# Layer 0's second half in one fixed order: retention, out-projection, norm and routing woven together, GpSimd's arithmetic moved to VectorE

## The chip, the core and the metric

The kernel runs on one core of a Trainium2 chip. The time is that of one execution on the device, in microseconds. Five engines work side by side, each on its own queue: TensorE (PE, with its weight loads as PEld), VectorE (DVE), ScalarE (ACT), GpSimd (POOL) and SyncE (SP), which only issues transfers. They wait for one another through semaphores.

## The reference

Two layers of a block with 256 context and 1024 latent tokens of width 1024; each has a mixer, a residual sum, a norm and a mixture of 32 experts. The part that matters here is layer 0 behind its in-projection: retention in both directions over chunks of 128 tokens and 4 heads, its group norm with a gate, the out-projection, the residual, the second norm and the router's choice of two experts for every token.

```python
scores = einsum('bhnid,bhnjd->bhnij', q, k) * dmat
inner  = einsum('bhnij,bhnje->bhnie', scores, v)
out    = inner + einsum('bhnid,bhnde->bhnie', q_dec, s_prev)   # s_prev: state before the chunk
s      = g_chunk * s + einsum('cd,ce->de', k * w_tail, v)      # from chunk to chunk
y  = (o - mean(o)) * rsqrt(var(o) + EPS) * gn_w * silu(gate)   # by head
x  = x + g1 * (concat([y, fourier_mix(f)]) @ w_out)
h2 = rms_norm(x, norm2_w) * (1 + sc2) + sh2
# router: softmax and argmax over 4 groups, top 2 of 8 experts in the group, for h2
```

## The kernel before

The ten token tiles (two of context, eight latent) are at the same time the ten chunks of the retention. Layer 0's first half (layer0_a, inproj0) computes q, k, v, gate and the Fourier part, and runs the backward retention, whose states it stores (SB_d). The second half, `layer0_b` (line 828), is a loop over steps s, in which three things are called one after the other for three neighbouring tiles: `ret_chunk` for chunk s, `outproj` and `out_norm` for tile s - 1, `router` for tile s - 2, and `route_part` after tiles 2, 5, 7 and 9.

`ret_chunk` (line 894) loads k, v, q, gate, Fourier part and backward state; GpSimd scales q for both directions (qd, line 907); PE forms the scores (sc), DVE multiplies them by the decay (sm); PE adds the products with the states and with v (o); PE transposes k, DVE scales it (kd), PE forms kv, and DVE updates the forward state SF, which the next chunk needs. DVE takes mean and variance of o by head (bn_stats, bn_aggr), forms the inverse square root by integer arithmetic and three Newton steps (`rsqrt_steps`, line 280), and normalizes (y, line 931); PE transposes y, DVE multiplies by the gate, and `mix_split` writes each factor as a rounded part (mh) and a residue (ml).

`outproj` multiplies mh and ml by the split weights: two halves of 512 columns, 24 products each, the four Fourier pieces first. DVE scales by the modulation g1 (yg, line 973) and GpSimd adds x (line 974). `out_norm` squares on ACT, has a second inverse square root on DVE, then h = x * r * A2 on DVE (line 988) and + S2 on GpSimd (line 989), and stores h2, from which the experts gather their rows. `router` transposes x, multiplies by the router's weights (lgp), and scales the logits by the same r; `route_part` turns the logits of two or three tiles into lists for the experts: many small DVE operations and a few small matmuls (rk, ls).

The order of the instructions on each engine is left to the framework's scheduler: it takes what its model says is ready, earlier calls first. Layer 1's first part does it otherwise: there `Ordered` (line 105) keeps PE, DVE and ACT in the order of the calls and keeps a model of the engines' times (`cost`, line 118), and `Weave` (line 208) runs several generators in steps between the products: at each `pump` it takes the first part by priority whose next step is ready by that model, and `until` lets PE's modelled time pass when none is. The experts (`moe`) follow layer 0's second half; their first gather needs the lists of the last `route_part`.

Of the kernel before, what the change touches and what calls it, by code (L numbers as in the profile page):

```python
# [19 lines left out]
P = 128  # L20
D = 1024
# [80 lines left out]
class Ordered:  # L102
# [13 lines left out]
    def cost(self, eng, op, out, ins, func):  # L116
        n = int(np.prod(out.shape[1:]))
        if eng != "tensor":
            n = max([n] + [int(np.prod(x.shape[1:])) for x in ins])
        if eng == "tensor":  # L120
            return max(n, 128 if ins[0].dtype == F32 else 64) * (2 if ins[0].dtype == F32 else 1) / 2400
        if eng == "vector":
            wide = any(x.dtype in (F32, F32R, I32) for x in [out, *ins])
            return 0.067 + n / 960 * (1.0 if wide else 0.5)
        if eng == "scalar":
            c = 0.02 + n / 1060
            if func is not None and func not in self.PLAIN and func != self.table:
                self.table = func
                c += 1.3
            return c  # L130
        return 0.2 + n / 480
# [128 lines left out]
class Emit:  # L260
# [565 lines left out]
            self.nc.vector.scalar_tensor_tensor(out=new[:, h, :], in0=old[:, h, :], scalar=self.gch[:, 4 * d + h:4 * d + h + 1], in1=kv[:, h, :], op0=OP.mult, op1=OP.add)  # L826

    def layer0_b(self):
        tc, nc, t = self.tc, self.nc, self.t
        pool = lambda s, **k: s.enter_context(tc.tile_pool(reuse_waits="tile", **k))  # L830
        with ExitStack() as st:
            b1 = pool(st, name="b1", bufs=1)
            wk = pool(st, name="wk", bufs=2)
            ps = pool(st, name="bps", bufs=1, space=PSUM)
            self.SF = None
            m, o = {}, {}
            for s in range(12):
                if s < 10:
                    m[s] = self.ret_chunk(wk, ps, s)
                if s == 0:  # L840
                    drain(self.load_wout(b1, t["even_w_out"][0], self.wsc, (2,)))
                    self.mid_setup(0, b1)
                if 0 < s < 11:
                    drain(self.out_rows(0, wk, 1 if s < 3 else 0))
                    x = self.outproj(0, wk, ps, s - 1, *m.pop(s - 1))
                    drain(self.out_norm(0, wk, s - 1, x))
                    o[s - 1] = x
                if s > 1:
                    drain(self.router(0, wk, ps, s - 2, o.pop(s - 2), s - 2, 1 if s < 4 else 0))
                    if s - 2 in (2, 5, 7, 9):  # L850
                        drain(self.route_part(ps, *{2: (0, 3, "kv"), 5: (3, 3, "kv"), 7: (6, 2, "kv"), 9: (8, 2, "sc")}[s - 2]))
        self.b0.close()
        self.hst.close()

# [36 lines left out]
        self.modset = self.rset = None  # L891
        self.rn = {}

    def ret_chunk(self, wk, ps, n):

        nc = self.nc
        v = nc.vector
        kT, vv = self.load_kv(self.wk0, n)
        qT = self.chunk_T(self.wk0, self.qT_d, n, "qT")
        gT = self.chunk_T(self.wk0, self.gT_d, n, "gT")  # L900
        fT = self.chunk_T(self.wk0, self.yT_d, n, "fT")
        SB = self.flat(self.wk0, self.SB_d[n], "SBt") if n != 1 else None
        SF = self.SF
        qd = self.wk0.tile([P, 2, 4, P], F32, name="qd", tag="qd", bufs=1)
        for d, S in ((0, SF), (1, SB)):
            if S is not None:
# [5 lines left out]
        v.tensor_tensor(out=sm, in0=sc, in1=self.DS, op=OP.mult)  # L912
        o = ps.tile([P, 4, P], F32, name="o", tag="o")
        for h in range(4):
            l = [(qd[:, d, h, :], S[:, h, :]) for d, S in ((0, SF), (1, SB)) if S is not None] + [(sm[:, h, :], vv[:, h, :])]
            for i, (a, b) in enumerate(l):
                nc.tensor.matmul(o[:, h, :], lhsT=a, rhs=b, start=(i == 0), stop=(i == len(l) - 1))
        if n < 9:
            kv = self.ret_kv(self.wk0, ps, kT, vv, 0)
# [3 lines left out]
        s6 = wk.tile([P, 4, 6], F32, name="s6", tag="s6")  # L923
        mv = wk.tile([P, 4, 2], F32, name="mv", tag="mv")
        for h in range(4):
            v.bn_stats(out=s6[:, h, :], in_=o[:, h, :])
            v.bn_aggr(out=mv[:, h, :], in_=s6[:, h, :])
        r = self.rsqrt(wk, mv[:, :, 1], 4, "gn")
        y = wk.tile([P, 4, P], F32, name="y", tag="sm", bufs=2)
        for h in range(4):  # L930
# [5 lines left out]
        return self.mix_split(wk, gT, fT)  # L936

    def mix_split(self, wk, a, b):
        nc = self.nc
# [53 lines left out]
    def router(self, layer, wk, ps, i, x, n, which):  # L993

        nc = self.nc
        v = nc.vector
        if self.rset != which:
            self.rset = which
            self.wra, self.rk = self.wr, self.rb
            if layer == 0:  # L1000
                self.wra, self.rk = self.modp.tile([P, KD, 36], F32, name="wra"), self.modp.tile([P, 36], F32, name="rk")
            lg = ps.tile([P, 36], F32, name="lgk", tag=self.tags["lg"][0], bufs=self.tags["lg"][1])
            for k in range(KD):
                nc.tensor.matmul(lg, lhsT=self.S2c[:, layer, which, k:k + 1].to_broadcast([P, P]), rhs=self.wr[:, k, :], start=(k == 0), stop=(k == KD - 1))
# [12 lines left out]
        for k in range(KD):  # L1017
            nc.tensor.matmul(lg, lhsT=xT[:, k, :], rhs=self.wra[:, k, :], start=(k == 0), stop=(k == KD - 1))  # L1018
        v.scalar_tensor_tensor(out=self.lgt[:, i, :], in0=lg, scalar=self.rn.pop(n), in1=self.rk, op0=OP.mult, op1=OP.add)
# [1308 lines left out]
```

## Time and profile before

| | us |
|---|---|
| three runs | 2817.58, 2820.12, 2822.80 (median 2820.12) |
| profiled execution | 2826.72 |
| its span | 2825.0 |
| PE busy | 2549.0 (90%) |
| DVE busy | 2282.9 (81%) |
| ACT busy | 1526.6 (54%) |
| POOL busy | 628.7 (22%) |
| mean granted clock of PE | 0.947 |

Times in the rows are counted from the span's start. A granted clock of 1.00 stands for 2.4 GHz and 0.50 for 1.2 GHz; a mean between them is a mixture. Matmuls overlap in the pipeline, so the pace of PE is read from one start to the next and not from the duration of one. A matmul of f32 operands appears as two instructions. In brackets stands how long the engine had been idle before an instruction, and who released it.

### The profile page before, as it was taken

Reading aid. Unit: us, or ns where it says so; the run is one execution under the profiler, and the core shown is the slowest. Engines: PE = TensorE matmul, PEld = TensorE weight load, DVE = VectorE, ACT = ScalarE, POOL = GpSimd, SP = SyncE. Lnnn points to the kernel's source line nnn. Section 1 sums busy time; section 2 is a strip of 40 time slices with the busy share of each in tenths; the row PEclk is TensorE's granted clock in tenths of the full one; section 3 lists DMA queues with packets and bytes.
Section 4 is the critical chain, followed back from the end, with each engine's and each line's share of the span. In section 5 each row is a group of like instructions: output and inputs, shape, how many; then the busy total and the mean of one; then the engine's idle time right before and its main releaser. Section 6 shows DMA issues by size and latency. Waiting matters only on the chain.

```text
span 2825.0 us, 40970 instructions
## 1 busy us (share of the span) xinstructions
PE 2549.0 (90%) x14733; PEld 2103.9 (74%) x14733; DVE 2282.9 (81%) x4243; ACT 1526.6 (54%) x2097; POOL 628.7 (22%) x543
## 2 busy tenths in 40 slices
PE   6999998986999999994899999989869999999980
PEld 3777787775778888883878788888757888888870
DVE  5688867676899999896858888487769999999877
ACT  3332121111778888884856644111227888888871
POOL 0001334333111222111213222113321111111114
PEclk8999999897999999997999999999969999999995
DMA  8455866334999999997636334785369999999884
GB/s 292 140 185 209 321 218 198 130 127 166 335 365 359 382 377 377 377 377 260 209 122 194 125 134 143 271 277 177 105 249 340 361 365 381 376 380 377 289 321 179
DMA packets 417356, 746.46 MB, mean 264 GB/s; under 512 B 50792, under 2 KB 137960, under 8 KB 414960
## 3 DMA queue, kind: packets, MB, share of 16 engines
q1 hardware_dynamic: 374688, 627.38, 63.9%
q0 software_dynamic: 41296, 112.10, 10.6%
q10 hardware_dynamic: 1152, 4.19, 0.4%
q8 instruction: 121, 1.98, 0.3%
q14 instruction: 99, 0.81, 0.1%
HBM read 667.69 MB, written 109.42 MB: 275 GB/s over the span
## 4 chain that ended last, share of the span: by engine, by line
issue 25%; PE 15%; DVE 5%; POOL 5%; DMA 4%; ACT 1%; POOLq 0%; SPq 0%; ACTq 0%; another core or an unknown queue 0%; DVEq 0%
PE acc L92 5%; POOL xe L1310 2%; POOL y_d L1314 1%; DMA y_d<-ye,sidx 1%; DMA kx<-kx_d 1%; PE tp L92 1%; PE tu L92 1%; PE op L324 1%; PE op L326 1%; PE op L322 1%; POOL y L92 1%; DMA y_d<-ye,v 1%; PE lgp L1018 1%; DVE cy L92 1%; PE rs L92 0%
## 5 line engine op out<-in xcount | busy, mean ns | idle before, releaser
L92 DVE TENSOR_TENSOR mwl<-mx,mwh 128x1024 fp32r<-128x1024 f32 x320 | 383.8, 1219 | 34.8 <-ACT mwh L92 32.5
L92 DVE TENSOR_TENSOR mwl<-raw,mwh 128x1024 fp32r<-128x1024 f32 x294 | 353.6, 1219 | 37.5 <-ACT mwh L92 36.3
L92 ACT ACTIVATE mwh<-mx 128x1024 fp32r<-128x1024 f32 x320 | 324.4, 1052 | 9.1 <-DMA h_d<-h 2.3
L92 ACT ACTIVATE mwh<-raw 128x1024 fp32r<-128x1024 f32 x294 | 298.2, 1051 | 8.3 <-DMA raw<-in_moe_w_gate 4.2
L92 PE MATMUL acc<-hUh,wr 128*128 128x512 f32 (+1 forms) x768 | 239.9, 389 | 0.8 <-ACT wr L92 0.6
L1310 POOL DMA_INDIRECT xe<-h_d,gidx x64 | 109.5, 1712 | 546.0 <-PE xt L92 516.5
L92 PE MATMUL u<-mwh,xTh 128*128 128x512 f32 x512 | 212.5, 415 | 0.0
L92 PE MATMUL g<-mwh,xTh 128*128 128x512 f32 x512 | 207.5, 405 | 0.0
L92 PE MATMUL g<-mwl,xTh 128*128 128x512 f32 x512 | 202.7, 396 | 3.7 <-DVE mwl L92 3.3
L92 PE MATMUL g<-mwh,xTl 128*128 128x512 f32 x512 | 201.5, 394 | 0.0
L92 PE MATMUL u<-mwh,xTl 128*128 128x512 f32 x512 | 201.4, 393 | 0.0
L1314 POOL DMA_INDIRECT y_d<-ye,sidx x64 | 98.2, 1534 | 460.3 <-ACT ye L92 429.6
L92 PE MATMUL u<-mwl,xTh 128*128 128x512 f32 x512 | 200.1, 391 | 0.0
L92 DVE TENSOR_TENSOR mwl<-mw,mwh 128x1024 fp32r<-128x1024 f32 x146 | 177.1, 1220 | 26.3 <-ACT mwh L92 25.6
L92 PE MATMUL dn<-mwl,aTh 128*128 128x512 f32 x496 | 193.8, 391 | 0.1
L92 PE MATMUL dn<-mwh,aTh 128*128 128x512 f32 x496 | 193.6, 390 | 0.0
L92 PE MATMUL dn<-mwh,aTl 128*128 128x512 f32 x496 | 193.1, 389 | 0.0
L433 DVE SCALAR_TENSOR_TENSOR adam<-raw,cs,adam 128x1024 f32<-128x1024 f32 x112 | 140.4, 1295 | 27.5 <-ACT adam L431 26.5
L92 PEld LDWEIGHTS acc<-hUh,wr 128*128 128x128 f32 x768 | 138.2, 191 | 22.3 <-ACT wr L92 0.8
L92 ACT ACTIVATE mwh<-mw 128x1024 fp32r<-128x1024 f32 x146 | 148.7, 1052 | 4.0 <-DMA mw<-in_moe_w_gate 2.2
L92 PE MATMUL acc<-hUl,wr 128*128 128x512 f32 (+1 forms) x384 | 148.7, 387 | 0.0
L322 PE MATMUL acc<-hTh,wh 128*128 128x512 f32 (+1 forms) x384 | 138.9, 362 | 0.0
(602 smaller groups left out, 6636.9 us busy)
## 6 DMA issues: line engine op xcount, KB each, us to landing
mx<-in_moe_w_up SPq DMA_DIRECT2D x62, 1024.0 KB
raw<-in_moe_w_up SPq DMA_DIRECT2D x56, 1024.0 KB
raw<-in_moe_w_down SPq DMA_DIRECT2D x55, 1024.0 KB
mx<-in_moe_w_gate SPq DMA_DIRECT2D x54, 1024.0 KB
raw<-in_moe_w_gate SPq DMA_DIRECT2D x50, 1024.0 KB
raw<-in_ada_w SPq DMA_DIRECT2D x48, 1024.0 KB
mx<-in_moe_w_down SPq DMA_DIRECT2D x41, 1024.0 KB
mw<-in_moe_w_down SPq DMA_DIRECT2D x37, 1024.0 KB
```

What stands on the lines that cost most here:

```text
L92: r = getattr(self.engine, op)(*a, **k)
L322: a = m(ps, lhsT=lh, rhs=rh, start=start, stop=False)
L324: b = m(ps, lhsT=lh, rhs=rl, start=False, stop=False)
L326: c = m(ps, lhsT=ll, rhs=rh, start=False, stop=stop)
L433: nc.vector.scalar_tensor_tensor(out=box[i], in0=w[:, r], scalar=c, in1=box[i], op0=OP.mult, op1=OP.add)
L1018: nc.tensor.matmul(lg, lhsT=xT[:, k, :], rhs=self.wra[:, k, :], start=(k == 0), stop=(k == KD - 1))
L1310: self.gath = nc.gpsimd.indirect_dma_start(out=x, out_offset=None, in_=h2, in_offset=bass.IndirectOffsetOnAxis(ap=idx, axis=0), bounds_che ...
L1314: nc.gpsimd.indirect_dma_start(out=self.y2_d, out_offset=bass.IndirectOffsetOnAxis(ap=idx, axis=0), in_=y, in_offset=None, bounds_check=2 ...
```

## The change

`layer0_b` now runs under `Ordered` and `Weave`: the retention (priority 1), the loading of a weight piece (2), the norm (3) and the routing (4) become generators, and the loop over the tiles calls only `outproj`, with the weave's `pump` between its products. Chunk n + 1 may begin when tile n's products begin. What GpSimd computed (qd, the sum with x, the sum with S2) is computed by DVE; kd and y move from DVE to ACT, four instructions of 128 columns each. For tiles 0 to 7 the second norm's inverse square root rides as a fifth column in that of the retention two chunks later. The square's unused output becomes a bf16 scratch tile. The modelled cost of a matmul in `Ordered.cost` is raised: f32 products to twice what they were, f32r products by 13 ns, others by 3; layer 1 uses the same function.

```diff
@@ cost
-            return max(n, 128 if ins[0].dtype == F32 else 64) * (2 if ins[0].dtype == F32 else 1) / 2400
+            if ins[0].dtype == F32:
+                return max(n, 128) * (2 if op == "transpose" else 4) / 2400
+            return max(n, 64) / 2400 + (0.013 if ins[0].dtype == F32R else 0.003)
@@ layer0_b
+        nc = self.nc = Ordered(self, tc.nc)
+        wv = Weave(nc)
-            for s in range(12):
-                if s < 10:
-                    m[s] = self.ret_chunk(wk, ps, s)
-                if s == 0:
-                    drain(self.load_wout(b1, t["even_w_out"][0], self.wsc, (2,)))
-                    self.mid_setup(0, b1)
-                if 0 < s < 11:
-                    drain(self.out_rows(0, wk, 1 if s < 3 else 0))
-                    x = self.outproj(0, wk, ps, s - 1, *m.pop(s - 1))
-                    drain(self.out_norm(0, wk, s - 1, x))
-                    o[s - 1] = x
-                if s > 1:
-                    drain(self.router(0, wk, ps, s - 2, o.pop(s - 2), s - 2, 1 if s < 4 else 0))
...
+            def rets():
+                ld = {0: self.ret_load(0)}
+                for n in range(10):
+                    if n + 1 < 10:
+                        ld[n + 1] = self.ret_load(n + 1)
+                    yield from self.ret_steps(wk, ps, n, *ld.pop(n), m, mv)
+                    yield lambda n=n: n <= state["at"]
+                    yield
+
+            def norms():
+                for n in range(10):
+                    yield lambda n=n: n in o
+                    yield
+                    if n > 7:
+                        yield from self.rsqrt_tile(wk, n, mv)
+                    yield lambda n=n: n in self.rn
+                    if n in (0, 2):
...
+                    yield from self.h2_steps(wk, n, o[n])
+
+            def routes():
+                for n in range(10):
+                    yield lambda n=n: n in o
+                    yield
+                    yield from self.router(0, wk, ps, n, o[n], n, 1 if n < 2 else 0)
+                    if n in (2, 5, 7, 9):
+                        yield from self.route_part(ps, *{2: (0, 3, "lg"), 5: (3, 3, "lg"), 7: (6, 2, "lg"), 9: (8, 2, "lg")}[n])
+            self.mid_setup(0, b1)
+            ret = wv.start(rets(), 1)
+            wo = wv.start(self.load_wout(b1, t["even_w_out"][0], self.wsc, (2,)), 2)
+            norm, route = wv.start(norms(), 3), wv.start(routes(), 4)
+            for n in range(10):
...
+                wv.until(lambda: n in m)
+                if n == 0:
+                    wv.finish(wo)
+                state["at"] = n
+                x = self.outproj(0, wk, ps, n, *m.pop(n), wv.pump)
...
+                nc.scalar.activation(junk, x, AF.Square, scale=1.0 / 32, accum_out=ss)
+                o[n] = x
+            wv.finish(ret, norm, route)
@@ ret_chunk -> ret_steps (generator; a yield names what the next step waits for)
-                nc.gpsimd.tensor_tensor(out=qd[:, d], in0=qT, in1=self.rowd[:, d], op=OP.mult)
+            v.tensor_tensor(out=qd, in0=qT[:, None].to_broadcast([P, 2, 4, P]), in1=self.rowd, op=OP.mult)
...
+            for h in range(4):
+                nc.scalar.activation(kd[:, h], tp[:, h], AF.Copy, scale=self.wfb[:, h:h + 1])
...
+        yield o,
...
+        steps = self.rsqrt_steps(wk, mv[:, :, 1], 5, "gn")
+        r = yield from steps
+        if n >= 2:
+            self.rn[n - 2] = r[:, 4:5]
+        nmr = wk.tile([P, 4], F32, name="nmr", tag="nmr")
+        v.scalar_tensor_tensor(out=nmr, in0=mv[:, 0:4, 0], scalar=-1.0, in1=r[:, 0:4], op0=OP.mult, op1=OP.mult)
...
-            v.tensor_scalar(out=y[:, h, :], in0=o[:, h, :], scalar1=mv[:, h, 0:1], scalar2=r[:, h:h + 1], op0=OP.subtract, op1=OP.mult)
+            nc.scalar.activation(y[:, h, :], o[:, h, :], AF.Identity, scale=r[:, h:h + 1], bias=nmr[:, h:h + 1])
+        if n < 9:
             self.SF = wk.tile([P, 4, P], F32, name="SF", tag="SF")
             self.ret_step(self.SF, SF, kv, 0)
+        yield y, ("tp", 1)
@@ h2_steps
+        v.scalar_tensor_tensor(out=h2, in0=x, scalar=self.rn[n], in1=self.A2, op0=OP.mult, op1=OP.mult)
+        yield
+        v.tensor_tensor(out=h2, in0=h2, in1=self.S2, op=OP.add)
@@ outproj
-            nc.gpsimd.tensor_tensor(out=x[:, c], in0=y, in1=x[:, c], op=OP.add)
+            (v if layer == 0 else nc.gpsimd).tensor_tensor(out=x[:, c], in0=y, in1=x[:, c], op=OP.add)
```

## Rows read from the trace of the kernel before

**Rows 1.** Stretches of the span: busy time of each engine, clock, DMA
```profile
core 0: us, PE busy (x) PEld busy (x) DVE busy (x) ACT busy (x) POOL busy (x), PEclk, DMA share, GB/s
429.50:446.10 16.60, 14.12 (x86) 12.69 (x85) 14.49 (x39) 3.60 (x6) 3.84 (x4) 0.90 0.75 227
446.10:677.70 231.60, 206.81 (x1150) 176.97 (x1149) 168.05 (x609) 31.48 (x58) 82.41 (x62) 0.90 0.44 146
677.70:700.10 22.40, 11.41 (x69) 10.35 (x67) 15.82 (x72) 7.55 (x12) 7.49 (x8) 0.65 0.53 187
...
780.00:1270.00 490.00, 487.18 (x2307) 399.10 (x2306) 451.18 (x485) 408.03 (x485) 85.46 (x52) 1.00 1.03 373
1460.00:1820.00 360.00, 347.99 (x3487) 292.49 (x3487) 265.87 (x648) 185.92 (x345) 99.83 (x125) 1.00 0.51 169
```

**Rows 2.** Timeline of PE at the stage's head: start, us, what
```profile
429.49 1.05 PE L910 MATMUL sc<-qT,kT 128*128 128x128 f32 x8
430.38 0.39 PE L917 MATMUL o<-SBt,qd 128*128 128x128 f32 x2
...
436.55 0.72 PE L322 MATMUL op<-hTh,mh 128*128 128x512 f32 x1
```

**Rows 3.** Timeline of DVE at the stage's head
```profile
431.89 3.09 DVE L875 SCALAR_TENSOR_TENSOR wol<-raw,gw,woh 128x512 fp32r<-128x512 f32 x3
...
440.47 0.49 DVE L926 BATCH_NORM_STATS2 s<-o 128x6 f32<-128x128 f32 x2 [1.34 <-PE o L917]
...
442.44 1.23 DVE L958 SCALAR_TENSOR_TENSOR A<-A,h 128x1024 f32<-128x1024 f32 x1
...
445.35 1.37 DVE L931 TENSOR_SCALAR y<-o,mv,gn_y 128x128 f32<-128x128 f32 x4
```

**Rows 4.** Timeline of PE inside two tiles
```profile
545.25 0.63 PE L326 MATMUL op<-hTh,ml 128*128 128x512 f32 x1
...
546.53 0.63 PE L326 MATMUL op<-hTh,ml 128*128 128x512 f32 x1
...
569.97 0.39 PE L322 MATMUL op<-hTh,mh 128*128 128x512 f32 x1
...
574.73 0.39 PE L322 MATMUL op<-hTh,mh 128*128 128x512 f32 x1
577.17 0.30 PE L934 MATMUL tp<-ident,y 128*128 128x128 f32 x1 [2.05 <-DVE y L931]
```

**Rows 5.** Waits of PE from 428 to 700: us in total, times, longest
```profile
PE rk L1112 <- DVE raw L1109: 18.0, 4, 8.5
PE tp L934 <- DVE y L931: 14.2, 6, 3.3
```

**Rows 6.** Groups of DVE and POOL, 428 to 700: busy us, mean ns, idle before
```profile
L931 DVE TENSOR_SCALAR y<-o,mv,gn_y 128x128 f32<-128x128 f32 x40 | 13.8, 403 | 0.4
L295 DVE SCALAR_TENSOR_TENSOR n_x<-n_y,n_h 128x1 f32<-128x1 f32 x30 | 9.2, 305 | 0.6
L286 DVE TENSOR_SCALAR gn_x<-mv 128x4 f32<-128x4 f32 x10 | 7.3, 734 | 0.3
L815 DVE TENSOR_TENSOR kd<-tp,wfb 128x512 f32<-128x512 f32 x9 | 6.1, 680 | 0.0
L974 POOL TENSOR_TENSOR x<-yg,x 128x512 f32<-128x512 f32 x20 | 27.7, 1387 | 102.4 <-DVE yg L973 96.9 <-issue 3.7 <-DVE raw L1109 1.7
L907 POOL TENSOR_TENSOR qd<-qT,rowd 128x512 f32<-128x512 f32 x17 | 25.6, 1524 | 35.3 <-PE o L917 35.3
L989 POOL TENSOR_TENSOR h<-h,S 128x1024 f32<-128x1024 f32 x10 | 23.8, 2383 | 20.1 <-DVE h L988 15.3 <-DVE raw L1097 4.8
```

**Rows 7.** Timeline of the tail: last product, a DVE operation, first gather
```profile
677.32 0.63 PE L326 MATMUL op<-woh,ml 128*128 128x512 f32 x1
...
685.73 2.05 DVE L1082 TENSOR_TENSOR raw<-lgt,raw 128x8 f32<-128x8 f32 x1
...
700.09 1.22 POOL L1310 DMA_INDIRECT xe<-h_d,gidx  x1 [8.73 <-DVE gidx L1263]
```

**Rows 8.** Timeline of ACT in layer 1: four pieces of 128 columns
```profile
1330.66 1.49 ACT L92 ACTIVATE xn<-tp,Sc,Ac 128x128 f32<-128x128 f32 x4
```

More of the change, by code (lines that the diff above doesn't have):

```diff
@@ new lines, in layer0_b @@
+            for n in range(2):
+                mv[n] = wk.tile([P, 5, 2], F32, name="mv", tag="mv", bufs=3)
+                nc.vector.memset(mv[n][:, 4], 1.0)
+            def rets():
[6 more added lines that the diff above has]
+                    yield
@@ L852, in layer0_b @@
+            wv.finish(ret, norm, route)
+        self.nc = tc.nc
         self.b0.close()
@@ L892, in mid_setup, with ret_load, ret_steps @@
         self.rn = {}
-    def ret_chunk(self, wk, ps, n):
+    def ret_load(self, n):
+        w = self.wk0
+        kT, vv = self.load_kv(w, n)
+        qT = self.chunk_T(w, self.qT_d, n, "qT")
+        SB = self.flat(w, self.SB_d[n], "SBt") if n != 1 else None
+        fT = self.chunk_T(w, self.yT_d, n, "fT")
+        gT = self.chunk_T(w, self.gT_d, n, "gT")
+        return kT, vv, qT, SB, fT, gT
+    def ret_steps(self, wk, ps, n, kT, vv, qT, SB, fT, gT, mix, mvs):
         nc = self.nc
         v = nc.vector
[L898 to L902, printed above, removed]
         SF = self.SF
+        mv = mvs[n]
+        yield kT, qT
         qd = self.wk0.tile([P, 2, 4, P], F32, name="qd", tag="qd", bufs=1)
-        for d, S in ((0, SF), (1, SB)):
-            if S is not None:
-                nc.gpsimd.tensor_tensor(out=qd[:, d], in0=qT, in1=self.rowd[:, d], op=OP.mult)
+        if SF is not None and SB is not None:
+            v.tensor_tensor(out=qd, in0=qT[:, None].to_broadcast([P, 2, 4, P]), in1=self.rowd, op=OP.mult)
+        else:
+            d = 0 if SB is None else 1
+            v.tensor_tensor(out=qd[:, d], in0=qT, in1=self.rowd[:, d], op=OP.mult)
         sc = ps.tile([P, 4, P], F32, name="sc", tag="sc")
@@ L912, in ret_chunk @@
         v.tensor_tensor(out=sm, in0=sc, in1=self.DS, op=OP.mult)
+        if n < 9:
+            yield kT, ("tp", 1)
+            tp = ps.tile([P, 4, P], F32, name="tp", tag="tp", bufs=2)
+            for h in range(4):
+                nc.tensor.transpose(tp[:, h, :], kT[:, h, :], self.ident)
+            kd = self.wk0.tile([P, 4, P], F32, name="kd", tag="kd")
+            for h in range(4):
+                nc.scalar.activation(kd[:, h], tp[:, h], AF.Copy, scale=self.wfb[:, h:h + 1])
+        yield sm, qd, vv, ("o", 1)
         o = ps.tile([P, 4, P], F32, name="o", tag="o")
@@ L917, in ret_chunk @@
                 nc.tensor.matmul(o[:, h, :], lhsT=a, rhs=b, start=(i == 0), stop=(i == len(l) - 1))
+            if h == 1:
+                yield
         if n < 9:
-            kv = self.ret_kv(self.wk0, ps, kT, vv, 0)
+            yield kd, ("kv", 1)
+            kv = ps.tile([P, 4, P], F32, name="kv", tag="kv", bufs=1)
+            for h in range(4):
+                nc.tensor.matmul(kv[:, h, :], lhsT=kd[:, h, :], rhs=vv[:, h, :], start=True, stop=True)
+        yield o,
+        s6 = wk.tile([P, 4, 6], F32, name="s6", tag="s6")
+        for h in range(4):
+            v.bn_stats(out=s6[:, h, :], in_=o[:, h, :])
+        for h in range(4):
+            v.bn_aggr(out=mv[:, h, :], in_=s6[:, h, :])
+        yield
+        steps = self.rsqrt_steps(wk, mv[:, :, 1], 5, "gn")
[4 more added lines that the diff above has]
+        v.scalar_tensor_tensor(out=nmr, in0=mv[:, 0:4, 0], scalar=-1.0, in1=r[:, 0:4], op0=OP.mult, op1=OP.mult)
+        y = wk.tile([P, 4, P], F32, name="y", tag="sm", bufs=2)
+        for h in range(4):
+            nc.scalar.activation(y[:, h, :], o[:, h, :], AF.Identity, scale=r[:, h:h + 1], bias=nmr[:, h:h + 1])
+        if n < 9:
             self.SF = wk.tile([P, 4, P], F32, name="SF", tag="SF")
             self.ret_step(self.SF, SF, kv, 0)
[L923 to L930, printed above, removed]
-            v.tensor_scalar(out=y[:, h, :], in0=o[:, h, :], scalar1=mv[:, h, 0:1], scalar2=r[:, h:h + 1], op0=OP.subtract, op1=OP.mult)
+        yield y, ("tp", 1)
         tp = ps.tile([P, 4, P], F32, name="tp", tag="tp", bufs=2)
@@ L935, in ret_chunk, with rsqrt_tile, h2_steps @@
         v.tensor_tensor(out=gT, in0=tp, in1=gT, op=OP.mult)
-        return self.mix_split(wk, gT, fT)
+        yield ("mh", 1),
+        mix[n] = self.mix_split(wk, gT, fT)
+    def rsqrt_tile(self, wk, n, mv):
+        self.rn[n] = yield from self.rsqrt_steps(wk, mv[n], 1, "n2")
+    def h2_steps(self, wk, n, x):
+        nc = self.nc
+        v = nc.vector
+        h2 = wk.tile([P, D], F32, name="h2", tag="h2", bufs=1)
+        v.scalar_tensor_tensor(out=h2, in0=x, scalar=self.rn[n], in1=self.A2, op0=OP.mult, op1=OP.mult)
+        yield
+        v.tensor_tensor(out=h2, in0=h2, in1=self.S2, op=OP.add)
+        self.h2_st = nc.gpsimd.dma_start(self.h2_d[n * P:(n + 1) * P, :], h2)
     def mix_split(self, wk, a, b):
@@ L1018, in router @@
             nc.tensor.matmul(lg, lhsT=xT[:, k, :], rhs=self.wra[:, k, :], start=(k == 0), stop=(k == KD - 1))
-        v.scalar_tensor_tensor(out=self.lgt[:, i, :], in0=lg, scalar=self.rn.pop(n), in1=self.rk, op0=OP.mult, op1=OP.add)
+        v.scalar_tensor_tensor(out=self.lgt[:, i, :], in0=lg, scalar=self.rn[n], in1=self.rk, op0=OP.mult, op1=OP.add)
     def chunk_T(self, pool, src, n, tag, bufs=None):
```

19 lines of the change are left out of this document (15 added, 4 removed).

## The prediction, made before any run of the changed kernel

> **What bounds the kernel now.** I read four views, in this order. First the table of stretches [rows 1]: it cuts the span where the work changes hands. Layer 0's stage runs from the last in-projection product (429.5 us) to the last out-projection product (677.7), then a tail to the first gather of the experts (700.1). In its main stretch PE is busy 206.8 of 231.6 us, and its granted clock averages 0.90: some of it ran at 1.2 instead of 2.4 GHz. No other engine is near full there: DVE 168, GpSimd 82, ACT 31. Compare the stretch 1460 to 1820, layer 1's in-projection, whose order is already written by a weave: 348 of 360 us busy at clock 1.00. And the experts (780 to 1270): PE busy 487 of 490, so whatever starts them earlier arrives at the end unshortened.
>
> Second, the waits of PE [rows 5]: 18.0 us before the rank products of the routing (four parts; the last, 8.5 us, lies in the tail) and 14.2 us in six waits before the transposes of y, that is, for the end of the retention's norm on DVE. Third, PE's order inside a tile [rows 4]: the products come every 0.227 us (4.76 us from 569.97 to 574.73, 21 steps), and then PE stands 2.05 us for y, though the tile still had products to run, behind the transposes of y. So the idle time isn't lack of work but its place in the queue. The same rows show what follows such a pause: three products take 1.28 us at 545 (0.427 each, 1.2 GHz against 2.4). Fourth, the tail [rows 7]: 22.4 us of one serial chain.
>
> So the stage is bound by PE's work plus the gaps that its order leaves. Work at full clock: 206.8 x 0.90 = 186.1 us in the main stretch and 14.1 x 0.90 = 12.7 in the head [rows 1], 198.8 us for ten tiles, 19.9 a tile.
>
> **The change part by part.** The sum is made against the profiled execution, 2826.7 us for a span of 2825.0; it lies 6.6 above the median of the runs (2820.1), and I subtract that at the end.
>
> *The head.* Before, chunk 0's retention and the first products of tile 0 (those of the Fourier half, which wait for no retention) overlap: the first product starts at 436.55 [rows 2]. After, the loop calls the products only when chunk 0's whole mix has been emitted, and the order on PE is kept, so y's transposes stand ahead of every product. The chain: DVE ends the rope work at 431.9 (where the next group starts, rows 3); qd and sm, 0.68 each as any 512 columns [rows 6], give 433.3; 16 half-products of o at half clock, twice the 0.11 of rows 2, 3.5; statistics and square root 440.47 to 445.35 less the 1.23 of the A row between, 3.7 [rows 3]; one small operation 0.2; y on ACT 1.5 [rows 8]; transposes 0.6; gating, rounding and residue 0.7 + 0.6 + 0.7. That is 445.5. The four wol pieces (0.75 to 1 us each, rows 3) keep DVE too; I let one get in the way: 446.6. PE has by then done chunk 0's 32 half-products and 8 transposes, 40 x 0.11 = 4.5 us. Bounds: 445.5 (none in the way) and 449.5 (all four).
>
> *The main stretch.* Left are 198.8 - 4.5 = 194.3 us of PE work. The nearest row for a woven order is layer 1's stretch: 348/360 = 0.967 busy at full clock [rows 1]. 194.3 / 0.967 = 201 us, plus 2 us because the first products start at half clock after the thin head: the last product ends at 649.6 instead of 677.7. Bounds: dense (194.3, end at 641) and the pace of before (677.7).
>
> *What must fit under it: the chain.* Chunk n+1 starts only when tile n's products start, and must be done when they end. Its own length: sc 0.9, sm 0.7, o 2.7 (24 half-products), 3.9 to the scale, y 1.5, transposes 0.5, gating and split 2.0, with some 1.5 of hand-offs 13.7 us. DVE is one queue in a fixed order: waiting behind each product tile's evictions (yg and x, 4 x 0.68), h2 (2 x 1.23), the state SF (1.4) and the routing (30 us over the ten tiles, an estimate) can add up to 9.6. So 14 to 23 us, against 19.9 of PE work. I take 19, the middle: the chain just fits.
>
> *GpSimd's work to DVE.* Removed are 27.7 (x), 25.6 (qd) and 23.8 us (h2) on GpSimd [rows 6]. DVE pays 20 x 0.68 = 13.6, 8 x 1.23 + 2 x 0.68 = 11.2 and 10 x 1.23 = 12.3 (1024 columns as the A row of rows 3), with the new small operation 1.7: 38.8 us. It gives back y 13.8 and kd 6.1 (to ACT), eight of the ten separate square roots (about 2.3 each, by the 0.3 of their steps: 18), and stalls: the first step of the retention's square root takes 0.73 on average [rows 6], where a step on as few columns takes 0.3 or less (n_x, same rows), because some of them stand while GpSimd adds h2. That is some 5 on this line and by estimate 10 to 20 in all. Net DVE 168 + 38.8 - 37.9 - 15 = 154 us in some 203: not the bound, and this is what hides the added 38.8. If the cover were gone (DVE late at each tile) it would be 9 x 1 us for every us.
>
> *y and kd on ACT.* Four pieces of 128 columns from PSUM take 1.49 us on ACT [rows 8]; four y took 13.8/10 = 1.38 on DVE. So the chain grows by 0.1 a tile, and ACT, at 31 of 232 us, takes 27 us more without notice. The Trainium skill speaks against this move: "ScalarE: Activation LUTs", Rules for kernel authors, sends plain adds and multiplies to VectorE, and its section on ACT_TABLE_LOAD prices an ACTIVATE with two pointer operands at 372 + 0.833 N ns, overlapping by 93; by that four y would be 1.64 us (an estimate), 0.26 more than on DVE, 2.3 us over nine tiles if the chain set the pace. The row gives 1.0 us for the same nine tiles; the chain rival below would end 1.3 us later by the page.
>
> *The queues.* The store of x and of h2 stay on GpSimd's queue and find it free. On SP the loads of chunk n+1 are issued a chunk earlier than used, as now; the S and A rows come after the norm's start instead of before the tile, and their first reader is h2, on no one's path. Cost 0; if an x load were late, 2 to 3 us once.
>
> *The tail.* x's last half on DVE instead of GpSimd saves 0.6 (1.39 to 0.68 and one hand-off); the 2.05 us operation at 685.73 [rows 7] is a stall beside GpSimd's h2 add and falls to 0.2, saving 1.8; h2's add now stands on DVE before the logits, -1.2; the slot indices come ahead of the gate values in the written order, +0.8. Sum -2.0; bounds +2 and -4.
>
> *Layer 1.* The changed cost line is also used by layer 1's weave: there the order changes without any change in work. PE's idle time there is 12 us of 360 [rows 1]; gone at best, doubled at worst. I take 0 and keep 8 each way.
>
> Sum: -28.1 - 2.0 = -30. 2826.7 - 30 - 6.6 = 2790 us.
>
> **The rivals.**
> *The chain sets the pace (0.22).* At 23 us a tile the last product ends at 446.6 + 9 x 23 + 12 = 665.6, gain 12 + 2: 2806. For it: the six waits for y now; the head adds 10 us before the first product. Against: 2 to 3 us of each wait came from stalls and a queue order that go.
>
> *The pauses cost the clock (0.08), the slower side.* If the chain takes more than some 24 us, PE stands 3.5 us before each tile as it does now in its longest waits, and half of the tile's 48 products run at 0.427 instead of 0.227: 20 + 3.5 + 4.8 = 28.3 us a tile, last product at 713, 33 us later: 2853. It decides from a tile of 24.6 us on, where the stage ends as before. The row at 545 shows the price; clock 1.00 in layer 1's woven stretch speaks against. The Trainium skill ("TensorE: Matmul & The Clock Gate", HAM oscillation) tells of loops whose every round begins throttled because each has its pause; by that rule this rival would be the rule as soon as each tile pauses.
>
> *The order brings nothing (0.06).* The gaps move, and only the relief of DVE counts: of the stalls next to none is PE's wait. 2826.7 - 6.6 - 4 = 2816, no change.
>
> *More than I count (0.08).* A dense stage and a better layer 1: 677.7 - 641 + 4 + 8 = 49, 2771. Against: the head, and DVE's fixed queue.
>
> **How the numbers follow.** Forecast 0.56, the others as given. A run of this kernel tells 0.2% (5.6 us) from no change. Faster: forecast, dense case and nearly all of the chain case, 0.85; same: 0.07; slower: 0.08. The range goes from the dense case to beyond the chain case with layer 1's 8 us against it: 2772 to 2812.
>
> **What would show it.** In the profile after: GpSimd computing nothing between 432 and the tail; first out-projection product near 447; y's transposes inside a run of products without a wait; last product near 650, clock 0.97 or more between; first gather about 20 us later; the stretch of the experts as long as now; layer 1's in-projection as long as now within 8 us. Wrong if the products of a tile come every 23 us or more (chain), if the clock in the stage falls below 0.9 (pauses), or if layer 1's stretch differs by more than 8.

## The result and the profile after

The change makes the kernel slower: 2836.91 us (median of five runs, 2835.97 to 2849.18) against 2818.83 (2816.09 to 2822.80) for the kernel before on the same chip; ratio 1.0076, 95% interval 1.0054 to 1.0098. I had said 2790, within 2772 to 2812. The profiled execution after is the longest of the five, 2849.18 us for a span of 2847.5 (2825.0 before: 22.5 us by the traces, 18 by the medians), so the traces are compared stage by stage. The profiled execution of e6 below ran at a much lower granted clock (0.82) than its other runs (0.94) and isn't read.

**Layer 0** gained, 20 us at the first gather where I had said 30. The rows below are the stretches of the kernel after, cut at the events of [rows 1]: end of the in-projection, first product, last product, first gather; then the experts.

```profile
core 0: us, PE busy (x) PEld busy (x) DVE busy (x) ACT busy (x) POOL busy (x), PEclk, DMA share, GB/s
429.50:445.60 16.10, 8.50 (x52) 6.69 (x50) 9.73 (x36) 5.61 (x13) 3.75 (x5) 0.88 0.64 212
445.60:643.30 197.70, 195.46 (x1172) 168.80 (x1172) 147.31 (x495) 52.13 (x125) 9.60 (x18) 0.98 0.49 161
643.30:680.00 36.70, 18.42 (x80) 17.16 (x80) 19.56 (x102) 4.61 (x11) 3.81 (x6) 0.55 0.48 175
780.00:1270.00 490.00, 485.24 (x2292) 395.75 (x2291) 444.56 (x462) 403.44 (x481) 82.90 (x51) 1.00 1.02 366
```

The products' stretch is dense (195.5 of 197.7 us at clock 0.98), GpSimd is down to issuing transfers (9.6 us), and the last product starts at 642.5 instead of 677.3 [rows 7]. The tail is longer, though: 36.7 instead of 22.4 us. The first gather comes at 680.0 instead of 700.1, 20 us earlier, and layer 1's first in-projection product is still 16 us earlier (1384.5 against 1400.5): the experts between took 704.5 us against 700.4, where they took 695 to 704 in the kernels below. Single traces of layer 0 scatter as well: e1 below has layer 0 as before, and there the last product starts at 671.3 and the first gather comes at 693.4.

The first rows below show GpSimd's former work and the scale of y on the engines that have them now (line, engine, operation, shapes, count, busy us, mean ns, idle before; compare [rows 6]). Below them is the head on PE, which waits 5.77 us for y before its transposes:

```profile
L92 ACT ACTIVATE y<-o,nmr,gn_y 128x128 f32<-128x128 f32 x40 | 15.1, 459 | 61.7 <-DVE nmr L92 61.7
L92 DVE TENSOR_TENSOR x<-yg,x 128x512 f32<-128x512 f32 x20 | 13.8, 692 | 0.7
L92 DVE TENSOR_TENSOR h<-h,S 128x1024 f32<-128x1024 f32 x10 | 12.2, 1218 | 0.0
L92 DVE TENSOR_TENSOR qd<-qT,rowd 128x1024 f32<-128x1024 f32 x8 | 9.7, 1218 | 0.0
```

```profile
444.00 1.53 PE L92 MATMUL tp<-ident,y 128*128 128x128 f32 x4 [5.77 <-ACT y L92]
445.57 0.79 PE L92 MATMUL op<-hTh,mh 128*128 128x512 f32 x1
```

**Layer 1** lost all of this and more. From that product to the first gather of its experts it took 688.6 us before (1400.5 to 2089.1) and 727.6 after (1384.5 to 2112.1). Two windows of PE, the first 200 us and the rest (us, busy, clock, DMA); first before, then after:

```profile
1400.50:1600.50 200.00, 190.18 (x1549) 0.99 0.47 150
1600.50:2089.10 488.60, 449.00 (x3699) 0.95 0.54 181
```

```profile
1384.50:1584.50 200.00, 176.61 (x1433) 0.93 0.44 140
1584.50:2112.10 527.60, 477.44 (x3815) 0.94 0.51 171
```

Busy time by clock is PE's work at full speed; what a window has beyond it is lost, by idling or by the low clock. Before: 200 - 190.18 x 0.99 = 11.7 and 488.6 - 449 x 0.95 = 62. After: 35.8 and 78.8. (The clock is printed to 0.01, so each has some 2 us of play.) The work is the same, 615 and 613 us; the 39 us are lost time, 24 in the first 200 us and some 17 later. The kernels below that have layer 1's written order of before (e2, e7, e9, e12, f3) lost 9 to 15 and 58 to 67 us by the same working, so both differences are clear of the scatter. These are some of PE's waits in the first 200 us (total, times, longest), before and after:

```profile
PE qn L92 <- ACT xr L92: 4.7, 3, 3.8
PE pq L92 <- ACT T L92: 0.5, 1, 0.5
```

```profile
PE pq L92 <- ACT T L92: 7.3, 3, 4.0
PE pq L92 <- DVE T L92: 3.9, 1, 3.9
PE qn L92 <- ACT xr L92: 3.6, 3, 2.1
PE tp L92 <- ACT cy L92: 3.4, 4, 1.1
```

pq is a step of the chunks' preparation (pq and tu form an inverse by doubling, and T is copied from PSUM between them); qn and cy belong to the convolutions of q, k and v. Now these steps stand among the products a little ahead of their inputs. Around each of the four longest pauses, 2.1 to 4.0 us, PE runs at 1.2 GHz (granted clock 0.50 from 1477.5 to 1482.9, behind the longest), and with one more such spell the clock is 0.93 instead of 0.99. The rule that I had cited for layer 0 (the Trainium skill, "TensorE: Matmul & The Clock Gate", HAM oscillation: every round of a loop pays for its pause with the clock) is told of a loop; the trace agrees for these single pauses, which are in layer 1 and not in layer 0 (clock 0.98).

Later the delta chain (products ks, av and others, ten chunks in two directions) ran partly among the out-projection's products before, at lines outside the weave; after, all of it (x144) lies under the in-projection. Rows of ks, before and after (count, ns min/median/max, first and last start):

```profile
L92 PE MATMUL ks<-S,kx x104: 271/275/377, 1798.8 to 1886.8; 128*128 128x128 f32 x104
L2196 PE MATMUL ks<-S,kx x40: 271/275/377, 1892.7 to 1973.2; 128*128 128x128 f32 x40
```

```profile
L92 PE MATMUL ks<-S,kx x144: 271/275/377, 1772.0 to 1896.9; 128*128 128x128 f32 x144
```

### The profile page after: what moved, and what is told of

It is laid out like the page before. It is cut to its first block, busy times and chain, and to the rows that moved or that the text cites. A ratio compares the mean times of both kernels' runs of the same rounds, so it can differ in the third digit from the quotient of the medians.

```text
span 2847.5 us, 40910 instructions
## 1 busy us (share of the span) xinstructions
PE 2559.5 (90%) x14733; PEld 2110.0 (74%) x14733; DVE 2270.0 (80%) x4166; ACT 1547.4 (54%) x2171; POOL 540.6 (19%) x495
## 4 chain that ended last, share of the span: by engine, by line
issue 26%; PE 12%; DVE 6%; POOL 5%; DMA 4%; ACT 2%; SPq 0%; POOLq 0%; DVEq 0%; ACTq 0%; another core or an unknown queue 0%
PE acc L92 3%; POOL xe L1404 2%; POOL y_d L1408 1%; DMA y_d<-ye,sidx 1%; DMA kx<-kx_d 1%; POOL y L92 1%; PE tr L92 1%; DMA y_d<-ye,v 1%; DVE dec L92 1%; PE su L92 1%; PE lgp L1112 1%; PE op L328 1%; PE op L326 1%; PE qs L92 1%; PE kq L92 1%
## 5 line engine op out<-in xcount | busy, mean ns | idle before, releaser
L92 PE MATMUL acc<-hUh,wr 128*128 128x512 f32 (+1 forms) x768 | 246.1, 395 | 0.6 <-ACT wr L92 0.6
```

Source lines behind the costliest of these rows:

```text
L92: r = getattr(self.engine, op)(*a, **k)
```

## The experiments

In every kernel "early" and "late" are PE's lost time in the first 200 us of layer 1's in-projection and from there to the first gather, worked out as above; "stretch" is the sum of both windows. Medians are of 5 to 12 runs, early and late of one profiled execution each; the ratio is to the kernel before on the same chip, and kernels of different chips are compared by it or by their traces.

| kernel | us | ratio (95%) | stretch | early | late |
|---|---|---|---|---|---|
| before (profile) | 2818.8 | 1 | 688.6 | 12 | 62 |
| after | 2836.9 | 1.0076 (1.0054 to 1.0098) | 727.6 | 36 | 79 |
| e1 before + line | 2859.1 | 1.0130 (1.0101 to 1.0158) | 723.2 | 32 | 78 |
| e2 old line in layer 1 | 2798.7 | 0.9916 (0.9883 to 0.9949) | 688.3 | 15 | 60 |
| e9 old line in both | 2814.9 | 0.9986 (0.9965 to 1.0006) | 691.8 | 13 | 66 |
| e3 f32 half only | 2809.8 | 0.9957 (0.9937 to 0.9976) | 691.6 | 17 | 65 |
| e4 fixed part only | 2814.3 | 0.9981 (0.9958 to 1.0004) | 699.9 | 30 | 58 |
| f1 new from the chain on | 2806.1 | 0.9951 (0.9933 to 0.9970) | 687.2 | 10 | 63 |
| f2 new up to the chain | 2832.2 | 1.0046 (1.0028 to 1.0064) | 720.9 | 36 | 75 |
| e5 chain held back | 2838.5 | 1.0093 (1.0061 to 1.0125) | 726.8 | 38 | 77 |
| e10 other engines slower | 2826.6 | 1.0026 (1.0000 to 1.0052) | 713.0 | 22 | 76 |
| e11 layer 1 "by trace" | 2829.7 | 1.0044 (1.0019 to 1.0068) | 722.3 | 24 | 88 |

**Is it the cost line?** e1 is the kernel before with only the line changed; e2 is the kernel after with the old line in layer 1.

```diff
- nc = self.nc = Ordered(self, self.tc.nc)            # layer 1, boundary
+ nc = self.nc = Ordered(self, self.tc.nc, False, False)   # e2: f32 and fixed part as before
...                                                  # the two flags in __init__ and cost
```

> The kernel before with nothing changed but the cost line of the weave (layer 0 stays as it was; only layer 1's written order can differ). Theory (the line costs layer 1 what layer 0 gains and more): the stretch from layer 1's first in-projection product to the first gather of its experts was 688.6 us before and is 727.6 after, so +39 here: about 2857 us, with the delta chain's last step ended before the out-projection. Rival (layer 0's own change slows layer 1, by what it leaves in buffers and queues): the line does nothing here, about 2819.

> The kernel after with the old cost line in layer 1's weave and the new one in layer 0's. Theory: layer 0's gain stays (first gather of its experts at 680 instead of 700, combine 18.5 us earlier) and layer 1 is back at 689 us: 2819 - 19 = about 2800 us. Rival (layer 0's change slows layer 1): 2837, as after.

Both came out as the theory said (2859.1 and 2798.7). The line alone costs 37 us, layer 0's part of the change alone gains 23, and the two nearly add (+13 against the +18 measured). The rival, that layer 0's change disturbs layer 1, is out: in e2 layer 1 is back at the windows of before.

```profile
1381.90:1581.90 200.00, 190.95 (x1514) 0.97 0.45 147
1581.90:2070.20 488.30, 441.86 (x3730) 0.97 0.54 182
```

**Which half of the line?** e3 keeps only the float32 factor of four, e4 only the fixed 13 and 3 ns, both in layer 1.

> The kernel after; in layer 1's weave only one half of the new cost line: float32 products at four times their columns instead of twice, and no fixed addition per product. In the trace float32 products of 128 columns follow each other every 0.13 us (nine in 1.17); the old line says 0.107, the new one 0.213, so this half is the wrong one and moves the modelled TensorE time by some 1100 x 0.107 = 118 us over layer 1. Theory (the doubling does the harm): 2830 to 2840 us, the delta chain again ended before the out-projection. Rival (the 13 ns per rounded product does it, some 1300 x 13 = 17 us): about 2800.

> The other half alone in layer 1's weave: the 13 ns (float32r) and 3 ns (others) per product, with the old cost of float32 products. In the trace the float32r products of 512 columns follow each other every 0.233 us; the old line says 0.213, the new one 0.226, so this half is the right one. Theory (the doubling does the harm): about 2800 us, at most 8 away from the kernel with the old line in layer 1. Rival: 2830 to 2840.

Neither is what either theory said: 2809.8 and 2814.3, 11 and 16 us above e2, together 27 of 38. The fixed part makes most of the early loss (30 against 15), and the late loss appears only with both (65 and 58 are within the 58 to 67 of the old order). The premise was wrong too, here and in e11 and f3: I counted rows, and a float32 product is two of them. The rows below are four products of chunk 0's o in the kernel after, with the state and with v in turn, at clock 1.00 (start, us):

```profile
435.51 0.49 PE L92 MATMUL o<-vv,sm 128*128 128x128 f32 x2
435.83 0.39 PE L92 MATMUL o<-SBt,qd 128*128 128x128 f32 x2
436.06 0.39 PE L92 MATMUL o<-vv,sm 128*128 128x128 f32 x2
436.28 0.39 PE L92 MATMUL o<-SBt,qd 128*128 128x128 f32 x2
```

A product every 0.22 to 0.23 us: the new line (0.213) is nearly right and the old (0.107) half of it. The fixed part is right as well: a float32r product of 512 columns starts every 0.233 us (nine from 1483.69 to 1485.79 in the kernel after), against 0.226 in the new line and 0.213 in the old. The line that costs 37 us is the truer one.

**Which place?** f1 uses the new line in layer 1 only from the delta chain's start on, f2 only up to it.

```diff
  def chain():
+     nc.f32 = nc.add = True      # f1; f2: False, with the new line before
```

> New line in layer 0 and, in layer 1, only from the start of the delta chain on; the preparation of the chunks is ordered by the old line. By the split of TensorE's lost time (24 us of the 40 in the first 200 us of the in-projection, 16 later) this kernel keeps the early stretch of the old line (lost 11 us) and loses the 16: layer 1's first in-projection product to the first gather 700 to 708 us (688 with the old line), total 2812 to 2820. Rival (the chain's part is harmless and the later loss was a consequence of the early order): 687 to 692 us, total 2796 to 2804.

> New line in layer 0 and, in layer 1, only up to the start of the delta chain; from there on the old line. By the split: lost time in the first 200 us 33 to 37 us as after (11 with the old line), later as with the old line; 708 to 716 us for the stretch, total 2820 to 2828. Rival (the later loss follows from the early order): 723 to 728 us, 2834 to 2840.

The rival is right in f1 by the stretch (687.2; the time, 2806.1, is 2 us over its range): the chain's own part is harmless. It is nearly right in f2 (720.9 and 2832, just under its range, far over the theory's). Windows of f1, then f2:

```profile
1383.10:1583.10 200.00, 192.15 (x1580) 0.99 0.47 154
1583.10:2070.30 487.20, 442.39 (x3666) 0.96 0.54 180
```

```profile
1378.60:1578.60 200.00, 176.53 (x1432) 0.93 0.44 140
1578.60:2099.50 520.90, 474.07 (x3816) 0.94 0.52 173
```

So nearly the whole loss (32 of 39 us) comes with the order up to the chain's start, most of the later part too. How the later part follows is argued: the preparation ends earlier (its last tu 355 us after the in-projection's first product, before the change 372), the chain starts earlier and is used up. In f2, as after, no ks is left for the out-projection (f1: 48 of 144), and there PE waits before the transposes of OF, the chain's result: 11.5 + 6.4 us by DVE's OF in f2, 11.0 + 4.1 after, 4.0 + 1.0 before, 7.6 + 1.6 in f1. But these waits alone don't settle it: e4 has 10.7 + 4.5 us of them, with 24 ks left, and a later loss of only 58.

e5 was meant to give this back by a later start of the chain (`s >= 17` instead of 12):

> The kernel after, new cost line in both layers; layer 1's delta chain may start only five in-projection units later (s >= 17 instead of 12), so that its last steps fall again among the out-projection's products. Theory A (all of the loss is that the chain is used up and the out-projection has no filler): at or below 2805 us. Theory B (the loss is in two places; out-projection and what follows hold some 13 of the 39 us, the rest are TensorE's waits and the lower clock in the first 140 us of the in-projection, where the preparation of the chunks stands too early): 2820 to 2828, with the stretch from 60 to 140 us after the first in-projection product still 64 to 69 us busy of 80. Rival (holding it back only leaves TensorE idle at the end): 2837 or more.

The rival came out (2838.5). The early part is unchanged, as theory B said, but the late part too: the first ks came only 29 us later, counted from the in-projection's first product (417 against 388 us), the rest crowded under the last products, and 8 of 144 were left. It didn't make the condition that it was to test.

**Why does a truer line do harm?** e6 asks for inputs that are ready 2 us before PE's modelled time in layer 1; e10 makes the other engines' modelled times longer, as the trace has them; e11 does as e10, with the float32 figure that I took for true (0.127 us) and with layer 0's routing parts as in e7 below.

```diff
- return 0.067 + n / 960 * (1.0 if wide else 0.5)      # VectorE
+ return 0.067 + 0.8 * self.add + n / 960 * (1.0 if wide else 0.5)   # e10, e11: add 0.1 in layer 1
- c = 0.02 + n / 1060                                  # ScalarE
+ c = 0.02 + self.add + n / 1060
```

> The kernel after, new cost line in both layers; in layer 1's weave a step is emitted only where its inputs are ready 2.0 us before TensorE's modelled time (0 before). Theory B (the new line lets TensorE's modelled clock run ahead of the other engines, so steps stand too early): the waits pq <- T and tp <- cy shrink, the stretch from 60 to 140 us is 72 to 77 busy of 80 at clock 0.95 or more, and the time falls to 2810 to 2822. Rival (the place of the steps does not matter, the loss comes from the chain's early end alone): 2830 to 2840, since the chain still ends before the out-projection.

> The kernel after, new cost line in both layers; in layer 1 the modelled times of the other engines are raised too, by 0.08 us per VectorE and 0.1 us per ScalarE operation (in the trace 256 columns take 0.38 us on ScalarE and 0.41 on VectorE, the model has 0.26 and 0.33). Theory (what counts is TensorE's modelled pace against that of the engines that it waits for; the new line raised one of the two): TensorE's lost time in the first 200 us of the in-projection (23.5 idle and 11.8 by the clock, 11.3 in the kernel before) falls to 20 or less, and the time to 2812 to 2825. Rival (the times of the other engines don't matter): 2835 to 2840.

> The kernel with the last two routing parts apart; layer 1's costs all by the trace: float32 products of 128 columns 0.127 us (before 0.107, new line 0.213), the fixed 13 and 3 ns, VectorE +0.08 and ScalarE +0.1 us per operation. Theory (a model true to all engines keeps or beats the old order): 2785 to 2795 us. Rival (the old costs, all too small, were set together with the steps' rules, so any change costs): 2800 to 2815.

e6 took 2877.8 us, worse than either said. As I read it, 2 us on every step of a serial preparation add up to far more than the 36 us at stake; that isn't shown. e10 went the theory's way and stopped just short of its marks: the early loss fell from 36 to 22 (20 was the mark), the time to 2826.6 (2825 was the mark). So PE's modelled pace against that of the engines that it waits for has its part in the early loss; in the kernel before the model's figures for those engines were too short as well (256 columns take 0.38 us on ACT, the model has 0.26). But the late loss stayed: in e10 and e11 48 ks were left for the out-projection, and yet 76 and 88 us were lost, now with waits of ks for the load of kx (8.1 + 3.3 + 1.8 us in e10). So a used-up chain isn't needed for a late loss. e11 (2829.7) is over both of its ranges. Why e10, with truer figures for PE, DVE and ACT, doesn't come near the old order isn't settled; the rest of the weave's rules (which unit starts the chain, when steps are released) was not varied with it.

**Layer 0's own order.** e9 has the old line there too, f3 only the fixed part.

> The kernel after with the old cost line in both layers, so that only layer 0's weave itself is left of the change. Theory 1 (the new line was needed for layer 0's order): the last out-projection product later than 650 (642.6 with the new line there), 2805 to 2815. Theory 2 (the weave gains by itself; the line is not needed): last product at 640 to 646, 2795 to 2803.

> Old line in layer 1; in layer 0 only the fixed 13 and 3 ns per product, float32 products at twice their columns. With the whole new line there the last product of layer 0's out-projection was at 642.6 and the first gather at 680, with the old line 656 and 691. In the trace a float32 product of 128 columns takes 0.11 to 0.13 us, so the fixed part is the true one. Theory (the true part brings it): last product 641 to 646, about 2800 us. Rival (the doubling brings it, by placing steps early): last product 650 to 656, 2810 to 2815.

e9 went as theory 1 said, f3 as the rival (2815.5, half a us over its range; 0.9992, 0.9973 to 1.0012): with the old line the last product starts at 656.0 and the first gather comes at 691.4, with the fixed part at 651.6 and 690.1, with the whole new line (e2) at 642.6 and 680.1. By the first gather the weave alone is worth 9 us, the fixed part 1, the float32 factor 10. Only the last is clear of the scatter: the intervals of e9 and f3 hold 1, so their times aren't told from the kernel before, and the first gather of e1 came at 693.4 with no weave there. As I read it, steps must stand early here, since the chain from o to y has to fit into a tile, and in layer 1 the same factor, with the fixed part, puts them too early; that wasn't tested by itself.

e8 gives qd and the two adds back to GpSimd, otherwise as e2.

> The kernel with the old line in layer 1 and the new one in layer 0; in addition the decayed queries (qd), the add of x and the add of h2 in layer 0 go back to GpSimd, woven as they are. This measures what it is worth that GpSimd computes nothing. VectorE is relieved of some 37 us of 150; in the kernel before, its operation beside GpSimd's adds stood up to 2.05 us instead of 0.2. Theory (the weave does it, not the move: VectorE is not the bound): 2795 to 2806, the last product within 5 us of 642.6. Rival (GpSimd's slow operations lie in the chain from o to y and take back the gain): the last product at 655 or later, 2810 or more.

The rival came out: 2817.8 us (1.0002, 0.9980 to 1.0025), the last product at 663.3, the first gather at 687.5. VectorE had 37 us less to do, yet from 429.5 us to the first gather it was busy for 167.2 us against 176.7 in e2, 9.5 less. One of its operations, in e2 and then in e8 (ns min/median/max), and then e8 around one of them (start, us):

```profile
L92 DVE TENSOR_TENSOR ml<-fT,mh x10: 678/681/693, 447.6 to 627.4; 128x512 fp32r<-128x512 f32 x10
```

```profile
L92 DVE TENSOR_TENSOR ml<-fT,mh x9: 677/1198/2360, 455.6 to 637.0; 128x512 fp32r<-128x512 f32 x9
```

```profile
497.33 2.41 POOL L92 TENSOR_TENSOR h<-h,S 128x1024 f32<-128x1024 f32 x1 [4.95 <-DVE h L92]
497.33 0.68 DVE L92 TENSOR_TENSOR gT<-tp,gT 128x512 f32<-128x512 f32 x1
497.93 2.36 DVE L92 TENSOR_TENSOR ml<-fT,mh 128x512 fp32r<-128x512 f32 x1
```

ml has both inputs in SBUF. The five of the nine that ran beside one of GpSimd's adds (h, 2.39 us on average, or x, 1.29) took 1.20 to 2.36 us and ended 0.55 us after it; the four that met none took 0.68. yg, with one input in PSUM, takes 686 ns in both, and no more in the two that ran beside h.

**The tail.** e7 (on e2) runs the last two routing parts as a generator of their own, in the PSUM slot that kv leaves free; g1 and g2 are e2 and e7 once more, on one chip.

```diff
-   if n in (2, 5, 7, 9):
-       yield from self.route_part(ps, *{2: (0, 3, "lg"), ...}[n])    # ...: cut
+   state["rt"] = n
+   if n in (2, 5):
+       yield from self.route_part(ps, n - 2, 3, "lg")
+def parts():
+   for n in (7, 9):
+       yield lambda n=n: state["rt"] >= n
+       yield
+       yield from self.route_part(ps, n - 1, 2, "kv")
```

> The kernel with the old line in layer 1 and the new one in layer 0; in addition the last two routing parts of layer 0 run as a sequence of their own, in the PSUM slot that the last chunk leaves free, so that the router of tiles 8 and 9 no longer stands behind the routing part of tiles 6 and 7. There the logits of tile 9 came at 668.2, 25.6 us after the last product (642.6), and the first gather 11.7 us after them. Theory (the tail was lengthened by that order): logits at 653 to 657, first gather at 667 to 671 instead of 680, 9 to 13 us less: 2786 to 2790 us. Rival (VectorE's own work sets the tail): first gather at 677 to 680, 2796 to 2799. What speaks against: the rank products of the routing part now stand before the last product, which may wait for them some 4 us.

> The kernel with the new cost line in layer 0 and the old one in layer 1, on the same chip as the next: 2795 to 2803 us, first gather at 680.

> The same with the last two routing parts of layer 0 apart. Theory (the experts start earlier and nothing behind them waits for anything else): first gather at 668 to 670 and 9 to 13 us less than the kernel beside it. Rival (the experts' weights, whose loads start at the same time as before, are what they wait for): less than 4 us.

The tail of the kernel after and that of e7, on PE:

```profile
642.46 0.39 PE L92 MATMUL op<-woh,ml 128*128 128x512 f32 x1
647.57 1.09 PE L92 MATMUL rk<-raw 128*128 128x96 f32 x4 [4.72 <-DVE n_h L92]
655.52 1.92 PE L92 MATMUL ls<-raw 128*128 128x32 f32 x8 [3.26 <-DVE raw L92]
...
659.09 3.63 PE L92 MATMUL lgp<-wra,h2T 128*128 128x36 f32 x16
...
664.36 3.63 PE L92 MATMUL lgp<-wra,h2T 128*128 128x36 f32 x16
673.33 1.08 PE L92 MATMUL rk<-raw 128*128 128x96 f32 x4 [5.34 <-DVE raw L92]
```

```profile
642.30 0.55 PE L92 MATMUL rk<-raw 128*128 128x96 f32 x4
642.67 0.48 PE L92 MATMUL op<-woh,ml 128*128 128x512 f32 x1
...
649.42 3.61 PE L92 MATMUL lgp<-wra,h2T 128*128 128x36 f32 x16
...
662.06 1.09 PE L92 MATMUL rk<-raw 128*128 128x96 f32 x4 [5.68 <-DVE raw L92]
```

After, the logits (lgp) of tiles 8 and 9 stand behind the lists (rk, ls) of tiles 6 and 7; in e7 tile 9's come 15 us earlier. The first gather comes at 668.7 against 680.1 in e2, as expected; the time, 2790.9 (0.9918, 0.9886 to 0.9949), is 1 us over the theory's range. On one chip g2 took 2790.5 (0.9906, 0.9871 to 0.9941) against 2798.3 (0.9934, 0.9907 to 0.9960) of g1: 8 us, a little under the theory and clearly over the rival's 4 by the medians, though the intervals overlap; the first gathers there were at 670.9 and 678.3.

e12 adds to e7 that tile 0's Fourier products run before chunk 0's y is there.

> The kernel with the last two routing parts apart (old line in layer 1); in addition tile 0's 24 products of the Fourier half, which wait for no retention, run before the transposes of y of chunk 0. There TensorE stands 5.6 us before these transposes (at 436 to 441.7), and the first products run at half clock. Theory: the wait goes, first gather 5 to 9 us earlier than 668.7, 2782 to 2786 us. Rival (chunk 1's chain, which starts with tile 0's products, is what tile 1 waits for, and it can't start earlier): within 3 us of 2791.

The rival came out: 2792.1 (0.9896, 0.9865 to 0.9927). The first product came at 436.8 instead of 443.2, but the last at 649.6 instead of 642.7, and the first gather at 675.7; what held the later tiles isn't shown.

The fastest version is e7 (g2 is the same kernel), 0.8 to 0.9% below the kernel before.

## Why the prediction was wrong

The step that failed is the last of the sum, *Layer 1*: "gone at best, doubled at worst. I take 0 and keep 8 each way". It measured +39 in the trace and 37 alone (e1). I had seen that the line is shared and bounded its effect by PE's 12 us of idle time between 1460 and 1820 [rows 1]. That is no bound: in the same 360 us behind the first product (1444 to 1804) the kernel after idles for 33.7 us, nearly three times as long, at clock 0.97 instead of 1.00, and most of what was lost later (some 11 of 17 us) falls in the last 209 us before the gather, which weren't in the window. No rival had this: the slower side (0.08) stood for pauses in layer 0.

The other steps:

- *Head*: first product 446.6 predicted, 445.6 measured. All four wol pieces stood between the statistics and y, not one, and other links of the chain were shorter, so the agreement is luck in part. (The links as listed add up to 444.8, not 445.5.)
- *Main stretch*: 649.6 predicted, 643.3 measured; 195.5 us busy of 197.7, near my dense bound, clock 0.98. The gain was 34 instead of 28; against e1, where the old order's last product ended at 671.7, it is 28.
- *The chain just fits*: right. No wait for y of note after tile 0 (5.8 us, in the head). The two rivals on the pace and the pauses of layer 0 didn't happen.
- *GpSimd to DVE*: DVE was busy for 147.3 us in the products' stretch, 154 predicted. With my +0.9 for the moved work the stalls come out, by difference, at 168.1 + 0.9 - 147.3, some 22, where I took 15.
- *y on ACT*: 15.1 us for 40 pieces, 1.51 for four; the row said 1.49, the estimate from the Trainium skill ("ScalarE: Activation LUTs", What ACT_TABLE_LOAD costs) 1.64. The measurement stands with the row.
- *Tail*: -2 predicted, bounds +2 and -4; measured +14. I counted the operations of the old tail and not that routing, the lowest priority, comes to the last product with the lists of tiles 6 and 7 still to do, which the old order had done by then. e7 takes 11 of the 14 back.

With the line out of layer 1 the time was 2799 (e2), and with the tail mended as well 2791 (e7); that this meets the 2790 that I forecast for the change as it stood confirms nothing, since e7 is another kernel.

## What to carry to other kernels

A cost that an order is planned by is part of the kernel for every stage that shares it: give each stage its own, and count such an edit as unbounded by the idle time seen so far. A truer figure for one engine can make the order worse: alone it cost 37 us here, and with the other engines' figures made truer too (e10) only a part came back. When work is woven under products, look at what the lowest priority has left when the products end.

## What was unexpected of the hardware

Moving 37 us of elementwise work from VectorE to GpSimd (e8) relieved VectorE by 9.5 us: an operation with both inputs in SBUF stood until the GpSimd operation beside it had ended (ml, up to 2.36 us instead of 0.68), one with an input in PSUM did not (yg, 0.686 us in both). The Trainium skill says so ("SBUF — State Buffer", SBUF: two separate sides: one shared pair of ports, locked for a whole instruction), and the trace agrees for these two. The first step of the retention's square root, five columns and one input, stood too: 0.96 to 1.09 us in the six that ran beside qd, 0.16 in the three that met nothing. h = x * r * A2, with both inputs in SBUF, took 1.28 us in both kernels; in e8 none of the eight met a GpSimd operation.

With the same written order of layer 1, the last 209 us before the gather, summed over windows of 40 us, lost 19 us by the clock in the profile of before and 9 in that of e2: thin stretches differ that much from one execution to the next.
